# Token norms in a feature-major layer: sums and factors by transposes in place of products

## The chip, the cores and the metric

One NeuronCore of a Trainium2 chip runs the whole program. The metric is the device time of one execution in microseconds (us). Engines: TensorE (PE; its weight loads are shown apart, as PEld), VectorE (DVE), ScalarE (ACT), GpSimd (POOL) and SyncE (SP, which only issues DMAs here). Each engine works through its own queue in order and waits on semaphores for the others. The times of the kernel before are 2595.07, 2595.23 and 2595.78 us.

## What is computed

One encoder layer on 2048 prompt tokens and 64 sample tokens, in FP32, 1024 features wide. The two RMS norms at the end of the layer are what the change touches: one over the output of `w_o`, one over the residual sum.

```python
def rms_norm(x, g):
    xf = x.astype(jnp.float32)
    y = xf * lax.rsqrt(jnp.mean(xf * xf, axis=-1, keepdims=True) + EPS) * g.astype(jnp.float32)
    return y.astype(x.dtype)
...
    merged = jax.nn.sigmoid(gA) * yA + jax.nn.sigmoid(gB) * yB
    out = jnp.einsum('btd,de->bte', merged, w_o)
    x = x + rms_norm(out, g_post)
    gate = jax.nn.sigmoid(jnp.einsum('btd,de->bte', rms_norm(x, g_ple), w_ple_gate))
    x = x + jnp.einsum('btp,pd->btd', p.astype(x.dtype), w_ple_proj) * gate
```

Ahead of these stand a pre-norm with a large input projection, a gated short convolution (path A) and a chunked linear-attention scan (path B), whose outputs are gated and merged.

## The kernel before

Activations lie feature-major: 128 features on the partitions, tokens along the row. The 2112 tokens are worked in three blocks of 768, 704 and 640, each in two halves. A dense product of FP32 quality is made of three matmuls on numbers split into a high and a low part (lines 444 to 446 in the gates and in the paths, 595 to 597, 633 to 635 and 1223 to 1225 elsewhere); many of them are combined by one level of Strassen's scheme. The weights' high parts are made on ScalarE (L228, L275), their low parts on VectorE (L228) or reloaded from DRAM by SP (L276, L238).

A norm over features needs a sum over partitions. `final_norm` first adds the squares of the eight feature tiles into one tile `acc` (ScalarE squares, L732; VectorE adds, L733). `rms` is then called, once per norm, on one or two halves (`segs`):

- `col_rstd` (L711) multiplies each 128-token piece of `acc` as the stationary operand with a column of ones. The result is one column per piece in PSUM: tokens on the partitions, three columns for a half, for 384, 352 or 320 tokens alike, since pieces may overlap.
- `rstd_of` scales and adds eps on VectorE (L688), and raises to the power -1/2 on GpSimd (L691).
- `spread` (L702) multiplies each column, broadcast along the row, with the identity, so that every partition of the PSUM result holds the factor of each token.
- The result is copied out of PSUM: on ScalarE (L724) in the first two blocks, on VectorE (L722) in the last.

`final_norm` then rescales x by it (L1366), adds the residual (L1367), and after the second norm makes the split operands of the last product (L1384, L228). In the first two blocks each norm takes both halves at once, while TensorE works on the next block's gates (L444 to L446; their evictions include L458, L464, L473, L485 and L492, the sigmoids L853 and L859, and the stores L866 on GpSimd's queue). In the last block each half has its norms by itself. `spread` is also called twice at the head of the program, on row sums of x that were made without `col_rstd` (copies at L1536).

PSUM has two pools of one-bank tiles: five for the dense products (`pg`) and three for attention and small work (`pa`); the sums and the spreads take `pa` tiles. The order of the work within a queue is set by a scheduler from priorities and modelled costs; `placed()` asks that an instruction be issued behind the last matmul of a group, and `behind_all` behind given instructions. `T.transpose` is used already in the attention (L1068, L1070, L1156).

Of the kernel before, what the change touches and what calls it, by code (L numbers as in the profile page):

```python
# [10 lines left out]
F32 = mybir.dt.float32  # L11
# [3 lines left out]
ALU = mybir.AluOpType  # L15
# [3 lines left out]
P = 128  # L19
D = 1024  # L20
# [73 lines left out]
def hybrid_step(  # L94
# [17 lines left out]
    V, A, G, T, SP = nc.vector, nc.scalar, nc.gpsimd, nc.tensor, nc.sync  # L112
# [3 lines left out]
    const = ctx.enter_context(tc.tile_pool(name="const", bufs=1))  # L116
# [34 lines left out]
    def hn():  # L151
        return width[0] // 2

    def rt(n=0, dt=F32):
        t = ring.tile([P, BN + 2], dt, tag="r", name=nm("r"))
        return t if n is None else t[:, : n or width[0]]
# [4 lines left out]
    def ps_attn():  # L161
        return psa.tile([P, 512], F32, tag="pa", name=nm("pa"))
# [13 lines left out]
        T.matmul(unread[:, :P], idle, idle, start=True, stop=True)  # L176
    ident = const.tile([P, P], F32, tag="ident", name="ident")
    make_identity(nc, ident)
    ones = const.tile([P, 1], F32, tag="ones", name="ones")
    V.memset(ones, 1.0)  # L180
    mhalf = const.tile([P, 1], F32, tag="mhalf", name="mhalf")
    V.memset(mhalf, -0.5)
    vec = const.tile([P, 9, KB], F32, tag="vec", name="vec")
# [114 lines left out]
    def placed():  # L298

        return tc.issue_after(last[0]) if last[0] is not None else nullcontext()  # L300
# [35 lines left out]
    def kept_w(i1, i2, name, anew=False, spread=False):  # L336

        keys = dict(A11=(i1, 0), A12=(i1, 1), A22=(i2, 1))
        if name in keys:
            return split_w(load_raw(w_blk[keys[name]]), None if anew else keys[name], spread)  # L340
        return split_w(load_raw(sums[i1][name]), (i1, name))
# [341 lines left out]
    def tiles_of(n):  # L683

        return [(i, min(i * P, n - P)) for i in range((n + P - 1) // P)]

    def rstd_of(ms_ap, out_ap, scale, start=0):
        scaled = V.tensor_scalar(out_ap, ms_ap, scale, EPS, ALU.mult, ALU.add).ins  # L688
        means[:] = [scaled]
        shape = [out_ap.shape[0], out_ap.shape[1]]  # L690
        powers[:] = [G.tensor_tensor(out_ap, out_ap, mhalf[start : start + shape[0], :].to_broadcast(shape), ALU.pow).ins]  # L691
        return scaled

    def cols_tile(n):
        return small.tile([P, (n + P - 1) // P], F32, tag="cols", name=nm("cols"))

    def spread(cols, n):

        pb = ps_attn()
        with placed():  # L700
            for i, o in tiles_of(n):
                T.matmul(pb[:, o : o + P], cols[:, i : i + 1].to_broadcast([P, P]), ident, start=True, stop=True)  # L702
        return pb[:, :n]

    def col_rstd(acc, n):

        pc = ps_attn()
        cols = cols_tile(n)
        with placed():
            for i, o in tiles_of(n):  # L710
                T.matmul(pc[:, i : i + 1], acc[:, o : o + P], ones, start=True, stop=True)  # L711
        rstd_of(pc[:, : cols.shape[1]], cols, 1.0 / D)
        return cols

    def rms(acc, out, segs, hasten=False):


        cols = [col_rstd(acc[:, cols_of(sg)], sg["n"]) for sg in segs]
        yield
        for sg, col in zip(segs, cols):  # L720
            if hasten:
                ahead[:] = [V.tensor_copy(out[:, cols_of(sg)], spread(col, sg["n"])).ins]  # L722
            else:
                A.copy(out[:, cols_of(sg)], spread(col, sg["n"]))  # L724
        yield
# [807 lines left out]
    with behind_all(done):  # L1533
        rs = rt()
        cols = [spread(ss[:, 0, 3 * h : 3 * h + 3], hn()) for h in range(2)]
# [30 lines left out]
    for bi, bl in enumerate(blocks):  # L1566
# [10 lines left out]
        cols, a_first = [], []  # L1577
# [16 lines left out]
        mg, xo, h2, acc = [], [], [], rt()  # L1594
# [117 lines left out]
```

## Time and profile before

| | |
|---|---|
| runs | 2595.07, 2595.23, 2595.78 us, median 2595.23 |
| span of the profiled execution, first to last instruction | 2590.9 us |
| median less span: what lies around it | 4.3 us |
| granted TensorE clock | 1.000 |
| busy: ScalarE | 1530.4 us, 59% |
| busy: GpSimd | 368.3 us, 14% |
| DMA, mean of 40 slices | 286 GB/s |

The execution's own time is not listed apart from the three runs; its span stands 4.3 us below their median. In the rows that follow, a line of the timeline has the start (us from the span's start), the duration, the engine, the line of the kernel, the operation, output and input, and a count where like instructions were merged; in brackets stands how long the engine had been idle, and whom it waited for. A listing of one line gives least, median and longest duration in ns. Matmul durations overlap, so the distance from start to start is what one costs.

### The profile page before, as it was taken

What the parts mean: (1) busy time and instruction counts of PE and PEld (TensorE: products, weight loads), DVE (VectorE), ACT (ScalarE), POOL (GpSimd) and SP (SyncE); (2) the same over time, 40 slices, a digit from 0 to 9 for tenths busy, and PEclk for the clock granted to TensorE, in tenths of its full rate; (3) what the DMA queues carried; (4) which work ended last, traced back from release to release, by engine and by line L of the source; (5) the groups of instructions that cost most, each with busy time, mean ns of one, the idle gap of its engine ahead of it and who ended that gap; (6) DMA issues with size and microseconds to landing.
All of it is one profiled execution on the core that took longest, in us unless ns stands there. A gap on an engine that the chain in (4) does not pass through costs nothing.

```text
span 2590.9 us, 47524 instructions
## 1 busy us (share of the span) xinstructions
PE 2572.4 (99%) x16436; PEld 2556.1 (99%) x16436; DVE 1726.9 (67%) x3500; ACT 1530.4 (59%) x2973; POOL 368.3 (14%) x677
## 2 busy tenths in 40 slices
PE   9999999999999999999999999999999999999999
PEld 9999999999999999999999999999999999999998
DVE  7788778888777775466464556987345545336967
ACT  6766676455453764466564555566456665446675
POOL 2011111230022021111111221102100000001011
PEclk9999999999999999999999999999999999999999
DMA  8678777899897888877768998989887788999986
GB/s 325 224 262 288 263 260 273 310 360 308 262 349 238 272 311 269 281 248 233 262 227 287 342 388 313 323 291 334 295 268 251 246 273 264 299 297 323 333 270 200
DMA packets 361234, 739.87 MB, mean 286 GB/s; under 512 B 44119, under 2 KB 48785, under 8 KB 360993
## 3 DMA queue, kind: packets, MB, share of 16 engines
q1 hardware_dynamic: 321696, 582.69, 67.3%
q0 software_dynamic: 39296, 154.14, 16.3%
q8 instruction: 129, 2.11, 0.3%
q14 instruction: 113, 0.92, 0.1%
HBM read 543.44 MB, written 193.22 MB: 284 GB/s over the span
## 4 chain that ended last, share of the span: by engine, by line
PE 90%; DMA 4%; DVE 4%; issue 1%; ACT 1%; SPq 0%; POOL 0%; DVEq 0%; ACTq 0%
PE pg L444 19%; PE pg L446 19%; PE pg L445 19%; PE pg L596 5%; PE pg L595 5%; PE pg L597 5%; PE pg L635 3%; PE pg L634 3%; PE pg L633 3%; PE pa L1098 1%; PE pa L1138 1%; DMA lo<-low 1%; PE pa L1140 1%; PE pa L1084 1%; DMA low<-lo 1%
## 5 line engine op out<-in xcount | busy, mean ns | idle before, releaser
L444 PE MATMUL pg<-r,hi 128*128 128x320 f32 (+2 forms) x3304 | 1086.4, 329 | 1.4 <-DVE r L492 0.7
L445 PE MATMUL pg<-r,hi 128*128 128x320 f32 (+2 forms) x3304 | 1067.6, 323 | 0.0
L446 PE MATMUL pg<-r,lo 128*128 128x384 f32 (+2 forms) x2356 | 768.8, 326 | 5.3 <-DMA lo<-low 3.4
L275 ACT CAST hi<-raw 128x512 fp32r<-128x512 f32 x730 | 449.7, 620 | 515.5 <-PE pg L445 179.2
L444 PEld LDWEIGHTS pg<-r,hi 128*128 128x128 f32 x3304 | 621.5, 188 | 3.3 <-issue 1.0
L445 PEld LDWEIGHTS pg<-r,hi 128*128 128x128 f32 x3304 | 621.9, 188 | 0.0
L446 PEld LDWEIGHTS pg<-r,lo 128*128 128x128 f32 x2356 | 442.5, 188 | 7.9 <-DMA lo<-low 4.4
L446 PE MATMUL pg<-r,s 128*128 128x352 f32 (+1 forms) x948 | 299.4, 316 | 0.3 <-DMA s<-low 0.3
L596 PE MATMUL pg<-r,hi 128*128 128x320 f32 (+2 forms) x864 | 277.4, 322 | 0.6 <-DVE r L228 0.6
L595 PE MATMUL pg<-r,hi 128*128 128x320 f32 (+2 forms) x864 | 275.0, 322 | 0.0
L228 ACT CAST hi<-raw 128x512 fp32r<-128x512 f32 x252 | 155.6, 620 | 155.5 <-PE pg L445 44.0
L228 DVE TENSOR_TENSOR r<-r,r 128x320 fp32r<-128x320 f32 (+7 forms) x354 | 208.7, 608 | 52.9 <-ACT r L228 51.3
L228 ACT CAST r<-r 128x320 fp32r<-128x320 f32 (+7 forms) x354 | 185.9, 557 | 57.0 <-DMA r<-w_blk 13.0
L228 DVE TENSOR_TENSOR lo<-raw,hi 128x512 fp32r<-128x512 f32 x231 | 157.9, 685 | 88.0 <-ACT hi L228 84.2
L597 PE MATMUL pg<-r,lo 128*128 128x352 f32 (+2 forms) x564 | 180.9, 321 | 0.7 <-DMA lo<-low 0.7
L446 PEld LDWEIGHTS pg<-r,s 128*128 128x128 f32 x948 | 177.9, 188 | 0.7 <-DMA s<-low 0.6
L228 ACT CAST hi<-s 128x512 fp32r<-128x512 f32 x156 | 96.2, 618 | 120.1 <-PE pg L445 102.0
L634 PE MATMUL pg<-r,hi 128*128 128x384 f32 (+2 forms) x512 | 166.8, 326 | 0.2 <-DVE r L228 0.2
L633 PE MATMUL pg<-r,hi 128*128 128x384 f32 (+2 forms) x512 | 166.3, 328 | 0.2 <-ACT hi L275 0.2
L596 PEld LDWEIGHTS pg<-r,hi 128*128 128x128 f32 x864 | 162.2, 188 | 2.4 <-DVE r L228 1.7
L595 PEld LDWEIGHTS pg<-r,hi 128*128 128x128 f32 x864 | 161.3, 188 | 1.3 <-ACT r L228 0.6
L458 ACT COPY hf<-pg 128x352 f32<-128x352 f32 (+2 forms) x354 | 157.1, 446 | 1.7 <-PE pg L446 1.3
(403 smaller groups left out, 4114.3 us busy)
## 6 DMA issues: line engine op xcount, KB each, us to landing
raw<-w_blk SPq DMA_DIRECT2D x577, 256.0 KB, 4.1
raw<-S SPq DMA_DIRECT2D x444, 256.0 KB, 4.2
lo<-low SPq DMA_DIRECT2D x422, 256.0 KB, 4.1
s<-low SPq DMA_DIRECT2D x308, 256.0 KB, 4.0
low<-lo SPq DMA_DIRECT2D x271, 256.0 KB, 3.8
S<-s SPq DMA_DIRECT2D x152, 256.0 KB, 3.6
low<-r POOLq DMA_DIRECT2D x54, 256.0 KB, 5.1
r<-w_blk POOLq DMA_DIRECT2D x52, 256.0 KB, 6.9
```

The lines of the kernel that those rows point to most:

```text
L228: return A.copy(hi, src).ins, V.tensor_tensor(lo, src, hi.bitcast(F32), ALU.subtract).ins
L275: A.copy(hi, raw)
L444: add(hi[:, k, :], xhi, start=start and k == 0, stop=False)
L445: add(hi[:, k, :], xlo, start=False, stop=False)
L446: last[0] = add(lo[:, k, :], xhi, start=False, stop=k == KH - 1).ins
L458: copied = A.copy(got[n], ps[bank])
L595: add(hi[:, k, :], xhi, start=start and k == 0, stop=False)
L596: add(hi[:, k, :], xlo, start=False, stop=False)
L597: last[0] = add(lo[:, k, :], xhi, start=False, stop=k == KH - 1).ins
L633: T.matmul(ps, hi[:, k % 4, :], xhi[:, c], start=k == ks[0], stop=False)
L634: T.matmul(ps, hi[:, k % 4, :], xlo[:, c], start=False, stop=False)
L635: last[0] = T.matmul(ps, lo[:, k % 4, :], xhi[:, c], start=False, stop=k == ks[-1]).ins
```

## The change

The sums over features no longer come from a product with ones. Each 128x128 piece of `acc` is transposed by TensorE into PSUM, so that tokens lie on the partitions and the partial sums of 128 features along the row, and VectorE adds along the row, three pieces in one instruction. `rstd_of` then reads and writes the small tile in SBUF in place of PSUM. The spread's product of a broadcast column with the identity becomes a transpose of the broadcast column. The tile of ones goes.

```diff
-    ones = const.tile([P, 1], F32, tag="ones", name="ones")
-    V.memset(ones, 1.0)
...
             for i, o in tiles_of(n):
-                T.matmul(pb[:, o : o + P], cols[:, i : i + 1].to_broadcast([P, P]), ident, start=True, stop=True)
+                T.transpose(pb[:, o : o + P], cols[:, i : i + 1].to_broadcast([P, P]), ident)
...
             for i, o in tiles_of(n):
-                T.matmul(pc[:, i : i + 1], acc[:, o : o + P], ones, start=True, stop=True)
-        rstd_of(pc[:, : cols.shape[1]], cols, 1.0 / D)
+                T.transpose(pc[:, i * P : i * P + P], acc[:, o : o + P], ident)
+        count = cols.shape[1]
+        V.tensor_reduce(cols, pc[:, : count * P].rearrange("p (i c) -> p i c", c=P), axis=mybir.AxisListType.X, op=ALU.add)
+        rstd_of(cols, cols, 1.0 / D)
         return cols
```

## The prediction

> **What bounds the kernel now.** I read the page first: busy shares by engine, then the chain that ended last.
>
> ```profile
> PE 2572.4 (99%) x16436; PEld 2556.1 (99%) x16436; DVE 1726.9 (67%) x3500; ACT 1530.4 (59%) x2973; POOL 368.3 (14%) x677
> PE 90%; DMA 4%; DVE 4%; issue 1%; ACT 1%; SPq 0%; POOL 0%; DVEq 0%; ACTq 0%
> ```
>
> TensorE is busy 99% of the span and 90% of the chain; VectorE has a third of its time free. So time taken off TensorE's queue shortens the run, and time put on VectorE costs only where TensorE comes to wait for it. Matmul durations overlap, so I price TensorE by the distance between starts, on the row of weight loads, and look at each place where a norm is made. There are seven stretches: H, the head (two spreads of the already finished row sums); A1 and A2, the two norms of the first block (each two sums, then two spreads); B1 and B2 of the second block; and in the third block four single norms C1 to C4 in order of time, each of one half of the tokens.
>
> ```profile
> L711 PE MATMUL pa<-ones,r x72: 164/250/271, 911.9 to 2545.6; 128*128 128x1 f32 x72
> L702 PE MATMUL pa<-ident,cols x72: 270/275/376, 915.1 to 2549.6; 128*128 128x128 f32 x72
> ```
>
> The listing of one line shows 72 records for L711; the code issues 36 products there, so an FP32 product is two records. L702 has 36 too, and 6 more in the head. 78 products become transposes.
>
> **Removed: the price of a product against a transpose.** Weight loads in A2 (start, duration, line):
>
> ```profile
> 958.03 1.47 PEld L711 LDWEIGHTS pa<-ones,r 128*128 128x128 f32 x12
> 959.41 0.19 PEld L444 LDWEIGHTS pg<-r,hi 128*128 128x128 f32 x1
> 959.52 0.19 PEld L445 LDWEIGHTS pg<-r,hi 128*128 128x128 f32 x1
> 959.69 0.19 PEld L446 LDWEIGHTS pg<-r,s 128*128 128x128 f32 x1
> ```
>
> From 958.03 to 959.52 lie six products and one ordinary matmul (0.16 to 0.17): 1.49 - 0.16 = 1.33 us, 0.222 each. The trace of before holds transposes of the same size in the attention (L1156, one record each):
>
> ```profile
> 123.79 0.53 PEld L1156 LDWEIGHTS pa<-ident,r 128*128 128x128 f32 x4
> 124.29 0.19 PEld L444 LDWEIGHTS pg<-r,hi 128*128 128x128 f32 x1
> 124.40 0.19 PEld L445 LDWEIGHTS pg<-r,hi 128*128 128x128 f32 x1
> 124.57 0.19 PEld L446 LDWEIGHTS pg<-r,lo 128*128 128x128 f32 x1
> ```
>
> Four transposes and one matmul (0.17) in 0.61: 0.44, or 0.11 each. Each edit saves 0.112 us, six save 0.67, three 0.34, and all 78 save 8.7. That is the most that TensorE can gain.
>
> A rule speaks against this: the Trainium skill, "TensorE: Matmul & The Clock Gate", Part 4: PE-mode transpose, gives about 275 ns for a 128x128 transpose inside a kernel, and says that transposes don't count as activity for the clock gate. If that were their spacing, the change would cost 78 x (0.275 - 0.222) = 4.1 us, an estimate from that page; the trace has starts 0.11 us apart, so by the row the rule's figure is a latency. No run here shows what a long row of transposes does to the clock; these come in threes and sixes among matmuls.
>
> **Added: a reduction on VectorE.** Twelve sums over three rows of 128, read from PSUM. The two nearest reductions, from SBUF:
>
> ```profile
> L1149 DVE TENSOR_REDUCE ms<-r 128x4 f32<-128x512 f32 x16 | 11.0, 687 | 27.9 <-ACT r L1148 27.9
> L1149 DVE TENSOR_REDUCE ms<-one 128x1 f32<-128x128 f32 x16 | 4.5, 279 | 0.0
> ```
>
> The second number behind the bar is the mean in ns. It is 408 ns for 384 more elements, so 384 take 279 + 272 = 551 ns. Bounds 0.28 and 0.69; I take 0.55. Twelve of them are 6.6 us of VectorE, nothing beside its 860 free, but each lies between the sums and the factors. `rstd_of` (scale on VectorE, power on GpSimd) stays, and so does the copy out of PSUM. The ones tile and its memset go, worth nothing: VectorE sets up while TensorE does its idle products.
>
> **Where the reduction meets TensorE.** In the changed program's order the queues are alike but for the places below. VectorE does reduce, reduce, scale, L473, scale, and at A1 and B1 GpSimd now issues one L866 store between its two powers. The second scale waits behind L473, which waits for a ScalarE copy (bound: nothing to 0.4). In SP's order five loads move by one to three places; I count that as nothing, covered by the weights already loaded for the matmuls ahead of them, and one stall of 2.9 (rival 2) is the price if that cover is gone. The spread waits for the power; behind it on TensorE stand the dense matmuls of the next gates, and for those the evictions on ScalarE and VectorE. A1:
>
> ```profile
> 911.86 1.42 PEld L711 LDWEIGHTS pa<-ones,r 128*128 128x128 f32 x12 [0.40 <-DVE r L733]
> 912.75 0.52 DVE L492 TENSOR_TENSOR r<-hf,hf 128x352 f32<-128x352 f32 x1
> 913.19 0.37 DVE L688 TENSOR_SCALAR cols<-pa 128x3 f32<-128x3 f32 x2
> 913.43 1.72 POOL L691 TENSOR_TENSOR cols<-cols,mhalf 128x3 f32<-128x3 f32 x2 [28.33 <-DVE cols L688]
> 915.11 0.61 POOL L866 DMA_DIRECT2D g__2774_11267<-r  x1
> ```
>
> Six transposes from 911.86 end at 912.52. VectorE is free at 913.19; two reductions end at 914.29; the power starts 0.24 behind the scale (913.43 - 913.19), lasts 0.86, and ends at 915.39; TensorE starts 0.05 later (as in C2 below, 2521.54 to 2521.59), 915.44. The new order has 13 matmuls before the first spread (11 before), at 0.161 each (A2: 963.24 - 958.03 less 1.33, over 24): 912.52 + 2.10 = 914.62, a wait of 0.82. Then the spread, 0.33, and five matmuls, 0.81: 916.58. The second power starts behind the store, 916.00, and is there at 916.91: 0.33 more. Of 1.34 saved, 1.15 is given back: -0.2.
>
> B1, with matmuls of 0.147 (C3: 2525.55 - 2523.11 less 0.67, over 12):
>
> ```profile
> 1758.78 1.41 PEld L711 LDWEIGHTS pa<-ones,r 128*128 128x128 f32 x12 [0.35 <-DVE r L733]
> 1759.04 0.48 DVE L492 TENSOR_TENSOR r<-hf,hf 128x320 f32<-128x320 f32 x1
> 1762.43 0.60 POOL L866 DMA_DIRECT2D g__5173_21796<-r  x1 [0.82 <-ACT r L859]
> ```
>
> VectorE is free at 1759.48 (0.44 behind that L492, as in A1), reductions go to 1760.58, power to 1761.69. The slot, ten matmuls behind the transposes, is 1758.78 + 0.66 + 1.47 = 1760.91: wait 0.82. The second power stands behind a store that waits for a ScalarE row. If that row comes 0.65 earlier with TensorE, the wait is 0.5; if not, 1.15. I take the first: net 0.0 (bound +0.6).
>
> B2, and the spread of A2:
>
> ```profile
> 1798.61 1.45 PEld L711 LDWEIGHTS pa<-ones,r 128*128 128x128 f32 x12
> 1800.88 0.22 DVE L688 TENSOR_SCALAR cols<-pa 128x3 f32<-128x3 f32 x2
> 963.24 1.46 PEld L702 LDWEIGHTS pa<-ident,cols 128*128 128x128 f32 x12
> 1803.47 1.45 PEld L702 LDWEIGHTS pa<-ident,cols 128*128 128x128 f32 x12
> ```
>
> In B2 VectorE comes to the sums only at 1800.88; reductions to 1801.98, first power to 1803.09. The slot moves up to 1802.80: wait 0.34, then 0.54 for the second power. Net -0.5. A2 has 5.2 us from 958.03 to 963.24, 4.5 after the change; sums 0.66, hand-over 0.22, reductions 1.1, 0.24, two powers 1.72: 4.0. No wait, -1.34.
>
> C2 and C3, by short windows of each engine:
>
> ```profile
> 2519.55 0.74 PEld L711 LDWEIGHTS pa<-ones,r 128*128 128x128 f32 x6 [0.31 <-DVE r L733]
> 2521.59 0.74 PEld L702 LDWEIGHTS pa<-ident,cols 128*128 128x128 f32 x6 [0.50 <-POOL cols L691]
> 2523.11 0.78 PEld L711 LDWEIGHTS pa<-ones,r 128*128 128x128 f32 x6
> 2525.55 0.78 PEld L702 LDWEIGHTS pa<-ident,cols 128*128 128x128 f32 x6
> 2520.42 0.16 DVE L688 TENSOR_SCALAR cols<-pa 128x3 f32<-128x3 f32 x1 [0.92 <-PE pa L711]
> 2520.66 0.88 POOL L691 TENSOR_TENSOR cols<-cols,mhalf 128x3 f32<-128x3 f32 x1 [18.89 <-DVE cols L688]
> 2524.09 1.00 DVE L1384 SCALAR_TENSOR_TENSOR r<-r,vec,r 128x320 f32<-128x320 f32 x2
> 2524.26 1.09 POOL L691 TENSOR_TENSOR cols<-cols,mhalf 128x3 f32<-128x3 f32 x1 [2.72 <-DVE cols L688]
> ```
>
> TensorE waits 0.50 here already. C2: the scale comes 0.33 sooner for the transposes and 0.55 later for the reduction, 2520.64; spread at 2521.81 instead of 2521.59, done at 2522.14 instead of 2522.26 with seven matmuls before it, not six. C3: six matmuls later transposes end at 2523.35, the reduction at 2524.12 (0.22 of hand-over, as 2520.42 stands behind the end of the sums at 2520.21). The new order then puts both L1384 (1.00) ahead of the scale: 2525.12, power 2525.36 to 2526.43, spread done at 2526.81 instead of 2526.22. The slot was 2523.35 + 13 x 0.147 = 2525.26, so TensorE waits 1.1. Less the two matmuls now done earlier (0.29), C2 and C3 lose 0.3 where they would have saved 1.34.
>
> C1 and C4 have slack:
>
> ```profile
> 2495.76 0.78 PEld L711 LDWEIGHTS pa<-ones,r 128*128 128x128 f32 x6
> 2499.07 0.78 PEld L702 LDWEIGHTS pa<-ident,cols 128*128 128x128 f32 x6
> 2545.05 0.74 PEld L711 LDWEIGHTS pa<-ones,r 128*128 128x128 f32 x6 [0.39 <-DVE r L733]
> 2548.91 0.78 PEld L702 LDWEIGHTS pa<-ident,cols 128*128 128x128 f32 x6
> ```
>
> After the change 3.0 and 3.5 us lie from sums to spread. C1 needs 0.33 + 0.22 + 0.55 + 0.24 + 0.88, and 0.5 for the L620 that the new order puts between reduction and scale (priced like one L1384): 2.7. C4 needs 2.4 with the power of 1.09. No wait, -0.67 each. The head has only spreads, no new chain: -0.67.
>
> **The sum:** H -0.67, A1 -0.19, A2 -1.34, B1 0.0, B2 -0.46, C1 -0.67, C2 with C3 +0.30, C4 -0.67: -3.7 us. The profiled span is 2590.9, the median of the runs 2595.2; the 4.3 around the span are not touched. So span 2587.2, time 2591.5.
>
> **The rivals.**
> (1) *Everything is kept.* The waits above rest on VectorE reaching the sums when it did before; where it is sooner, or the waits use up later ones, the whole 8.7 stays: 2586.5. For it: few TensorE waits for VectorE in the whole trace. Against: the 0.50 wait at 2521.59.
> (2) *Slower: the late factors block VectorE's queue.* The rescaling of x (L1366) waits for the spread, and evictions that free TensorE's PSUM banks stand behind it. It decides where lateness exceeds the bank slack. Price: the 1.2 us of A1 once more at A1, B1, B2 and C3, plus one more stall of weights like the longest of this group:
>
> ```profile
> PEld pg L446 <- DMA lo<-low: 4.4, 4, 2.9
> ```
>
> -3.7 + 4.8 + 2.9 = +4.0, 2599.2; with another such stall 2602. Against: the pool has five banks, and at A1 the new order puts the eviction L464 ahead of the first L1366, and L485 behind two of them instead of three.
> (3) *Transposes cost their duration.*
>
> ```profile
> L1156 PE MATMUL pa<-ident,r x112: 270/272/302, 124.0 to 2178.2; 128*128 128x128 f32 x112
> ```
>
> 0.272 is 0.05 more than a product: 78 x 0.05 = +3.9, 2599.1; the waits would be no longer than above, since TensorE comes to them later. It is the mechanism of the rule named above. The spacing of 0.11 speaks against it.
> (4) *It doesn't do what it says*: the compiled transposes of a broadcast column are two records as before. Then 42 spreads save nothing (4.7 us less): +1.0, 2596.2.
>
> **How the numbers follow.** Forecast 0.48, (1) 0.36, (2) 0.11, (3) 0.02, (4) 0.03. The likeliest is 2591.5. Its own unknowns: B1 +0.6, the reduction at 0.69 instead of 0.55 some +1.0 in five waits, at 0.28 some -2; one longer or vanished DMA stall 2.9: 2587 to 2596. Together with (1) the range is 2585.0 to 2598.0. The mark of 0.2% (what a measurement can tell from no change) is 5.2 us: faster means below 2590.0. (1) and the low edge of the forecast make 0.40; slower is (2) where the second stall of weights comes in, and what no case names, 0.10; 0.50 is left.
>
> **What would show it.** L711's successor and L702 with half as many records, starts 0.11 us apart. Twelve reductions near 0.55 us. TensorE waits for GpSimd of 0.8 and 0.3 at A1, the like at B1, 0.9 in C2, 1.1 in C3, none in A2. Wrong would be: reductions over 0.7 us, no such waits (then rival 1), or new waits of TensorE for evictions within 15 us behind A1 and B1 (rival 2).

## The result, and the profile after

| | before | after |
|---|---|---|
| runs of this comparison, median | 2595.23 us (2594.28 to 2596.14, 5 runs) | 2584.25 us (2581.3 to 2587.84, 5 runs) |
| ratio after to before | | 0.9968, 95% interval 0.9956 to 0.998 |
| span of the profiled execution | 2590.9 us | 2579.6 us (its time: 2581.3, the fastest of the five) |

The change makes the kernel faster, by 11.0 us between the medians. The forecast was 3.7 us, and the median lies 0.75 us below the low edge of the range. The recorded ratio, 0.9968, is not the quotient of these two medians, which is 0.9958: by the ratio the change is worth 8.3 us and the time is 2586.9, inside the range. The record does not say how the ratio was formed. Either way the kernel gained more than was forecast, so the question for the experiments is where the other 5 to 7 us come from.

The page of after, top lines and the chain that ended last:

```profile
span 2579.6 us, 47382 instructions
PE 2562.4 (99%) x16358; PEld 2546.4 (99%) x16358; DVE 1733.2 (67%) x3511; ACT 1529.9 (59%) x2973; POOL 369.5 (14%) x677
PE 86%; issue 5%; DVE 4%; DMA 3%; ACT 1%; POOL 1%; SPq 0%; DVEq 0%; POOLq 0%; ACTq 0%
```

TensorE has 78 records fewer (16436 less 16358): each of the 78 edits dropped one. VectorE has 6.3 us more, and 11 instructions more: twelve reductions less the memset of the ones. "issue" rose from 1% to 5% of the chain, which looks like lost time and isn't. The chain of after around A1 (start, duration, piece):

```profile
880.02 0.54 POOL r L1348
880.56 30.02 issue
910.58 0.02 POOLq L866
...
910.62 0.64 POOL cols L689
...
913.24 0.54 PE pa L700 x3
```

Going back from the spread (L700), the chain steps over to GpSimd, since TensorE waited for its power (L689), and then follows GpSimd's own queue back through 30 us in which GpSimd had nothing to do. TensorE worked through those 30 us. A like piece of 26.0 us stands ahead of B1; the two are some two thirds of the rise. What is new is that the chain steps over to GpSimd at A1, B1, B2, C2 and C3, where in before it did so at C2 alone.

The listings of the new lines in after (least, median, longest in ns):

```profile
L711 DVE TENSOR_REDUCE cols<-pa x12: 548/554/558, 909.4 to 2535.0; 128x3 f32<-128x384 f32 x12
L700 PE MATMUL pa<-ident,cols x36: 270/273/323, 911.8 to 2538.2; 128*128 128x128 f32 x36
L689 POOL TENSOR_TENSOR cols<-cols,mhalf x12: 845/1050/1107, 910.6 to 2535.8; 128x3 f32<-128x3 f32 x12
```

A reduction takes 0.55 us, and the spreads of the norms are 36 records where they were 72. What TensorE waits for, summed over the whole program, first in before and then in after (us in total, times, longest):

```profile
PEld pa L702 <- POOL cols L691: 0.5, 1, 0.5
```

```profile
PEld pa L700 <- POOL cols L689: 5.8, 8, 1.1
```

This is the price of the reductions: 5.3 us more of waiting for the factors. 78 edits at 0.112 are 8.7 us, less 5.3 is 3.4. The places, by weight loads of after at A1, B1, B2 and then C2 and C3:

```profile
908.11 0.64 PEld L709 LDWEIGHTS pa<-ident,r 128*128 128x128 f32 x6 [1.01 <-DVE r L733]
...
911.76 0.30 PEld L700 LDWEIGHTS pa<-ident,cols 128*128 128x128 f32 x3 [0.87 <-POOL cols L689]
...
913.24 0.30 PEld L700 LDWEIGHTS pa<-ident,cols 128*128 128x128 f32 x3 [0.42 <-POOL cols L689]
...
1753.21 0.30 PEld L700 LDWEIGHTS pa<-ident,cols 128*128 128x128 f32 x3 [0.90 <-POOL cols L689]
...
1754.70 0.30 PEld L700 LDWEIGHTS pa<-ident,cols 128*128 128x128 f32 x3 [0.48 <-POOL cols L689]
...
1793.55 0.30 PEld L700 LDWEIGHTS pa<-ident,cols 128*128 128x128 f32 x3 [0.38 <-POOL cols L689]
1794.59 0.30 PEld L700 LDWEIGHTS pa<-ident,cols 128*128 128x128 f32 x3 [0.74 <-POOL cols L689]
...
2511.01 0.30 PEld L700 LDWEIGHTS pa<-ident,cols 128*128 128x128 f32 x3 [1.06 <-POOL cols L689]
...
2515.59 0.30 PEld L700 LDWEIGHTS pa<-ident,cols 128*128 128x128 f32 x3 [0.94 <-POOL cols L689]
```

And A2, where nothing waits:

```profile
952.40 0.74 PEld L709 LDWEIGHTS pa<-ident,r 128*128 128x128 f32 x6
...
956.93 0.73 PEld L700 LDWEIGHTS pa<-ident,cols 128*128 128x128 f32 x6
```

To see what each stretch is worth, I compared the distance between the same two dense weight loads in both kernels. All kernels of this study have 16280 weight loads outside the sums and the spreads. They come in the same order, but for at most 30 that change places inside A1, B1 and C2 with C3, so at the bounds of every stretch the n-th load is the same piece of work. Differences to the profile of before shown above, in us, by the prediction's names. It counts seven stretches, but names nine places, and as C2 and C3 share one row here there are eight; they are called the norm stretches below, and the seven stretches in the expectations:

| stretch (time in before) | forecast | after | after, 2nd profile | after, 3rd profile |
|---|---|---|---|---|
| H (20 to 30) | -0.67 | -0.43 | -0.43 | -0.49 |
| A1 (908 to 925) | -0.19 | +0.42 | -0.22 | -0.21 |
| A2 (955 to 975) | -1.34 | -1.37 | -1.37 | -1.37 |
| B1 (1757 to 1772) | 0.0 | -0.15 | -0.09 | -0.17 |
| B2 (1797 to 1815) | -0.46 | -0.31 | -0.64 | -0.29 |
| C1 (2490 to 2503) | -0.67 | -0.65 | -0.67 | -0.67 |
| C2 and C3 (2517 to 2530) | +0.30 | +0.08 | +0.07 | +0.08 |
| C4 (2543 to 2553) | -0.67 | -0.64 | -0.62 | -0.62 |
| together | -3.7 | -3.0 | -4.0 | -3.7 |
| 545 to 582, no norm in it | 0 | -3.4 | -2.8 | -3.8 |
| all the rest, no norm in it | 0 | -4.9 | -0.8 | -2.5 |

The norms gave about what was forecast. The remainder of the first profile's 11 us lies where the two kernels do the same work in the same order on TensorE, and the largest piece of it is at 545 to 582. TensorE's waits there, of before and then of after:

```profile
PEld pg L446 <- DVE lo L228: 3.3, 5, 1.4
PEld pg L444 <- issue: 1.0, 1, 1.0
```

```profile
PEld pg L442 <- issue: 0.7, 1, 0.7
PEld pg L444 <- DVE lo L226: 0.2, 1, 0.2
```

In before TensorE waits five times for low parts of weights (L228, the same line as L226 in after); in after once.

### The profile page after: what moved, and what is told of

It reads as the page before. It is cut to its first block, busy times and chain, and to the rows that moved or that the text cites. A ratio compares the mean times of both kernels' runs of the same rounds, so it can differ in the third digit from the quotient of the medians.

```text
span 2579.6 us, 47382 instructions
## 1 busy us (share of the span) xinstructions
PE 2562.4 (99%) x16358; PEld 2546.4 (99%) x16358; DVE 1733.2 (67%) x3511; ACT 1529.9 (59%) x2973; POOL 369.5 (14%) x677
## 4 chain that ended last, share of the span: by engine, by line
PE 86%; issue 5%; DVE 4%; DMA 3%; ACT 1%; POOL 1%; SPq 0%; DVEq 0%; POOLq 0%; ACTq 0%
PE pg L442 18%; PE pg L443 18%; PE pg L444 18%; PE pg L594 4%; PE pg L593 4%; PE pg L595 4%; PE pg L633 3%; PE pg L632 3%; PE pg L631 3%; PE pa L1098 1%; PE pa L1138 1%; PE pa L1140 1%; PE pa L1084 1%; DMA lo<-low 1%; DVE lo L226 1%
## 5 line engine op out<-in xcount | busy, mean ns | idle before, releaser
L226 ACT CAST hi<-raw 128x512 fp32r<-128x512 f32 x252 | 155.5, 620 | 155.8 <-PE pg L443 40.0
L226 DVE TENSOR_TENSOR r<-r,r 128x320 fp32r<-128x320 f32 (+7 forms) x354 | 209.5, 611 | 51.9 <-ACT r L226 50.4
L226 ACT CAST r<-r 128x320 fp32r<-128x320 f32 (+7 forms) x354 | 185.8, 557 | 54.4 <-DMA r<-w_blk 10.9
L226 DVE TENSOR_TENSOR lo<-raw,hi 128x512 fp32r<-128x512 f32 x231 | 158.7, 689 | 86.8 <-ACT hi L226 81.5
L226 ACT CAST hi<-s 128x512 fp32r<-128x512 f32 x156 | 96.3, 618 | 123.9 <-PE pg L443 107.4
```

What stands on the lines that cost most here:

```text
L226: return A.copy(hi, src).ins, V.tensor_tensor(lo, src, hi.bitcast(F32), ALU.subtract).ins
```

## The experiments

Three groups of kernels ran, each with its own runs of before beside it; the median of before was 2591.2, 2589.3 and 2590.2 us, its single runs from 2584.8 to 2600.6. Every kernel has 12 timed runs and one profile. "Norms" is the sum over the eight norm stretches, "545" the stretch from 545 to 582, "rest" what is left of the difference at the last weight load; all three are us against the first profile of before. The expectations were written down with absolute times counted from the first comparison; since before is 4 to 6 us lower in these groups, only their differences can be held against the results.

| kernel | median (range), us | ratio to before, 95% interval | norms | 545 | rest |
|---|---|---|---|---|---|
| spreads alone | 2586.12 (2582.93 to 2589.83) | 0.998, 0.997 to 0.999 | -3.9 | -1.7 | -1.9 |
| sums alone | 2591.14 (2586.78 to 2595.91) | 0.9997, 0.9987 to 1.0006 | +1.5 | +0.5 | -1.2 |
| head kept as products | 2586.36 (2583.84 to 2591.65) | 0.9984, 0.9975 to 0.9993 | -3.3 | -3.6 | +0.8 |
| head alone | 2588.68 (2587.03 to 2595.88) | 0.9996, 0.9987 to 1.0005 | -0.6 | -0.9 | -3.1 |
| after again | 2586.27 (2581.05 to 2587.67) | 0.9983, 0.9973 to 0.9993 | -4.0 | -2.8 | -0.8 |
| before again | 2590.34 (2583.47 to 2594.44) | 1.000, 0.9987 to 1.0012 | +0.1 | -0.3 | -6.3 |
| mixed | 2583.17 (2579.56 to 2586.29) | 0.9976, 0.9966 to 0.9986 | -5.4 | -2.2 | -0.5 |
| each reduction twice | 2588.92 (2585.01 to 2592.52) | 0.9994, 0.9984 to 1.0004 | -3.2 | -0.8 | +1.3 |
| after, third | 2585.52 (2581.69 to 2590.11) | 0.9979, 0.9968 to 0.9991 | -3.7 | -3.8 | -2.5 |
| mixed again | 2583.77 (2580.28 to 2588.17) | 0.9975, 0.9965 to 0.9985 | -5.6 | -4.0 | -2.8 |
| before, third | 2592.42 (2587.97 to 2598.23) | 1.0006, 0.9996 to 1.0016 | +0.6 | -3.1 | +4.8 |

### Spreads alone

The factors by transposes, the sums by products with ones as in before.

```diff
-                T.transpose(pc[:, i * P : i * P + P], acc[:, o : o + P], ident)
-        count = cols.shape[1]
-        V.tensor_reduce(cols, pc[:, : count * P].rearrange("p (i c) -> p i c", c=P), axis=mybir.AxisListType.X, op=ALU.add)
-        rstd_of(cols, cols, 1.0 / D)
+                T.matmul(pc[:, i : i + 1], acc[:, o : o + P], ones, start=True, stop=True)
+        rstd_of(pc[:, : cols.shape[1]], cols, 1.0 / D)
```

> Only the spreads are transposes (42 of them); the sums stay products with ones, no reduction. By the prices of the prediction: 42 x 0.112 = -4.7 us at the norms, with no new wait of TensorE for GpSimd except a longer one in C2 (0.5 before). Theory S (the head, 0.7 us shorter, shifts all that follows, and the waits of TensorE between 545 and 580 us go with the shift): a further -3.4 us there, 2587 in all. Theory R (those waits come and go from run to run): at the head -0.7, between 545 and 580 nothing that holds in all runs, 2590.

TensorE's waits for the factors in this kernel:

```profile
PEld pa L702 <- POOL cols L691: 0.7, 2, 0.5
```

0.2 us more than in before, for 42 edits: 4.7 saved, less 0.2 of waits, less 0.2 at the head (below) is 4.3, and the norm stretches show 3.9. Half of the change already gives all that the whole change gives at the norms. The stretch from 545 to 582 came out at -1.7, between theory S (-3.4) and theory R, and does not decide between them.

### Sums alone

The reverse: sums by transposes and a reduction, spreads by products.

```diff
-                T.transpose(pb[:, o : o + P], cols[:, i : i + 1].to_broadcast([P, P]), ident)
+                T.matmul(pb[:, o : o + P], cols[:, i : i + 1].to_broadcast([P, P]), ident, start=True, stop=True)
```

> Only the sums are transposes with a reduction; the spreads and the head stay products. At the norms -4.0 by the transposes and about 3 given back in waits for GpSimd at A1, B1, B2, C2 and C3: -1. Theory S: no shift before A1, so the waits between 545 and 580 stay (4 us of them), 2594. Theory R: they may be gone in the profiled run though nothing ahead of them has changed.

```profile
PEld pa L700 <- POOL cols L689: 5.7, 8, 1.0
```

36 edits save 4.0 us, and 5.2 us of new waits are put in: +1.2, and the norm stretches show +1.5 (A1 +0.92, B1 +0.68, B2 +0.30, C2 and C3 +0.85, against A2 -0.69, C1 -0.33, C4 -0.29). The waits of the changed kernel belong to this half of the change. Its time is the same as before within its interval.

### The head: kept as products, and alone

The first kernel is after with the two spreads of the head as products; the second is before with those two as transposes.

```diff
-    def spread(cols, n):
+    def spread(cols, n, head=False):
...
+                if head:
+                    T.matmul(pb[:, o : o + P], cols[:, i : i + 1].to_broadcast([P, P]), ident, start=True, stop=True)
+                else:
...
-        cols = [spread(ss[:, 0, 3 * h : 3 * h + 3], hn()) for h in range(2)]
+        cols = [spread(ss[:, 0, 3 * h : 3 * h + 3], hn(), True) for h in range(2)]
```

> The changed kernel with its two spreads at the head made by products again; the six matmuls are all that differs. Theory S: the waits between 545 and 580 are back, 0.7 + 3.4 slower than the changed kernel in the profile, about 2588 to 2589 in the median. Theory R: 0.7 slower only, about 2585.

> The kernel before with only the two spreads at the head as transposes. Theory S: -0.7 at the head and -3.4 between 545 and 580, 2591. Theory R: -0.7, 2594.5.

Apart from the memset of the ones, the head's edit is the only part of the change ahead of 545 us, so if the change itself removed the waits at 545 to 582, this would have to be its cause. It isn't: without it that stretch is 3.6 us shorter, with it alone 0.9. Of the six spreads' 0.67 us at the head 0.43 arrive. The weight loads of after show why:

```profile
23.78 0.74 PEld L700 LDWEIGHTS pa<-ident,rows 128*128 128x128 f32 x6
24.67 0.19 PEld L1223 LDWEIGHTS pa<-r,r 128*128 128x128 f32 x1 [0.15 <-ACT r L1230]
```

The load behind the spreads now waits 0.15 us for a ScalarE row, for which no wait shows in before; that is most of the 0.24 that are missing.

### After again, before again

Both kernels unaltered, in one group.

> The changed kernel once more, unaltered. Theory P (the change is worth what it does at the norms; the first profile gained the rest in waits on DMAs that differ from run to run): about -3 at the norms in the trace again, a median some 3 to 5 us under the kernel before, and another sum in the stretches 545 to 582, 935 to 950, 1500 to 1535 and 1776 to 1790. Theory Q (the change itself removes those waits): 10 to 11 us under the kernel before, with the same four stretches as short as in the first profile.

> The kernel before once more, unaltered. Theory P: the four stretches differ from the first profile of it by some us in all, the norms by less than 0.1 us each; ratio 1.000. Theory Q: the four stretches are as in its first profile.

The norm stretches of after come out as in its first profile, but for A1 (+0.42 there, -0.22 here) and B2. But the same program of before, run again, ended 6.4 us sooner than in its first profile (span 2584.5 against 2590.9), with nothing changed at the norms (+0.1). So stretches outside the norms move by nearly as much as the whole surplus of the first comparison. One stretch shows it in both directions: 935 to 950 is 1.7 us shorter than in the first profile of before in after, 1.8 us longer in after again, and 1.9 us shorter in before again. TensorE's waits there are on transfers, in the first profile of before and in after again:

```profile
PEld pg L446 <- DMA lo<-low: 2.9, 1, 2.9
```

```profile
PEld pg L444 <- DMA lo<-low: 2.7, 1, 2.7
PEld pg L444 <- DMA s<-low: 0.5, 1, 0.5
```

The waits alone don't explain it: they are 2.9 us in the one and 3.2 in the other, and the stretch is 1.8 us longer. The rest goes with the granted clock of TensorE. 935 to 950 in each of the same two profiles' own time (window, length, busy time of each engine, then granted clock, DMA share and GB/s):

```profile
935.00:950.00 15.00, 12.40 (x77) 12.10 (x77) 11.46 (x16) 8.57 (x16) 2.69 (x5) 1.00 1.01 371
```

```profile
935.00:950.00 15.00, 12.40 (x66) 11.85 (x65) 9.93 (x15) 7.65 (x15) 2.16 (x4) 0.89 0.99 366
```

In after again the clock was halved for some 3.4 us, and matmuls there start 0.29 us apart, not 0.16:

```profile
941.31 0.49 PE L442 MATMUL pg<-r,hi 128*128 128x352 f32 x1
941.60 0.50 PE L443 MATMUL pg<-r,hi 128*128 128x352 f32 x1
```

That is about 1.5 us lost, an estimate from these two distances; with the 0.3 us more of waits it makes up the 1.8. Five of the thirteen profiles have such a dip in this stretch (after again, the third of before, sums alone, head kept as products, each reduction twice). In them the stretch is 1.0 to 2.1 us longer than in the first profile of before; in the other seven, at 1.00, it is 0.2 to 1.9 shorter. Two more dips stand elsewhere, at 576 in sums alone and at 1784 in each reduction twice. All seven begin within 1.4 us behind the end of a TensorE wait of 2.0 to 2.9 us. But five waits of 2.2 to 2.9 us have no dip behind them, that of the first profile of before among them, and what decides is not shown.

### Before and after for a third time

In two profiles of after the stretch from 545 to 582 had been short, and in two of before long. That left it open whether the change shortens it by a way that I had not seen.

> The changed kernel once more, unaltered, for a third profile. In two profiles of it the stretch from 545 to 582 us is 3.4 and 2.8 us shorter than in the first profile of before, in one further profile of before 0.3 us shorter. Theory P (what the change is worth is its seven stretches, 3 to 4 us; the rest is waits on transfers that differ from run to run): 3 to 4 us below the before of this call, the seven stretches again -3 to -4 together, 545 to 582 anywhere between 0 and -3.5. Theory Q (the change itself also removes the waits at 545 to 582): that stretch again 2.8 to 3.4 shorter, and 6 to 7 us below before.

> The kernel before once more, unaltered, for a third profile. Theory P: its stretch from 545 to 582 us falls anywhere between 0 and -3.5 against its first profile, and its span lies between 2584 and 2591. Theory Q: the stretch is long, within 0.5 us of the first profile, as in both profiles of before so far.

TensorE's waits at 545 to 582 in the third profile of before:

```profile
PEld pg L446 <- DVE lo L228: 1.0, 2, 0.5
PEld pg L444 <- issue: 0.7, 1, 0.7
```

The unaltered kernel before has the short stretch too: -3.1 us, with 1.0 us of waits for the low parts in place of 3.3. The change is not needed for it, and theory Q falls. Theory P did not come out whole either: the stretch of after, -3.8, lies just beyond its bound. In this profile of before C2 with C3 is 0.45 us longer, where TensorE waits 0.8 us for the last addition of squares (L733; 0.3 in the first profile), so sums over the norm stretches can differ by 0.6 with no edit at all. Elsewhere TensorE lost time to transfers, the clock dipped at 943, and the span was 2593.2, the longest of all and above the 2591 that theory P allowed:

```profile
PEld pg L446 <- DMA lo<-low: 4.6, 4, 2.9
PEld pg L597 <- DMA lo<-low: 3.7, 2, 2.2
PEld pg L446 <- DMA s<-low: 2.8, 5, 0.8
```

The span of before is 2590.9, 2584.5 and 2593.2 in three profiles, that of after 2579.6, 2583.4 and 2580.9.

### Each reduction twice

After with every reduction issued twice, which doubles its 0.55 us. The result is the same; the time is that of 24 reductions.

```diff
-        V.tensor_reduce(cols, pc[:, : count * P].rearrange("p (i c) -> p i c", c=P), axis=mybir.AxisListType.X, op=ALU.add)
+        for _ in range(2):
+            V.tensor_reduce(cols, pc[:, : count * P].rearrange("p (i c) -> p i c", c=P), axis=mybir.AxisListType.X, op=ALU.add)
```

> The changed kernel with every reduction done twice, into the same columns: 0.55 to 0.6 us more on VectorE between each sum and its factor, 1.2 where a norm has two. If the reduction sits on TensorE's path at A1, B1, B2, C2 and C3 and in slack at A2, C1 and C4: +1.2 at A1, +1.2 at B1, +1.2 at B2, +0.55 at C2 and at C3 each, 0 at C4, 0.3 to 0.6 at A2 and at C1, whose slack is about used up: some +5 in all. If VectorE's part is hidden everywhere: no site moves.

If the wait at a norm were the reduction's length alone, A1 and B1 would have grown, by 1.1 us each. They shrank: A1 is 0.60 us shorter than in before (0.2 in the second and third profiles of after), B1 0.86 (0.1 to 0.2). Weight loads of this kernel at A1, B1 and C1:

```profile
909.34 0.64 PEld L709 LDWEIGHTS pa<-ident,r 128*128 128x128 f32 x6 [0.37 <-DVE r L734]
...
913.72 0.30 PEld L700 LDWEIGHTS pa<-ident,cols 128*128 128x128 f32 x3 [0.49 <-POOL cols L689]
...
1759.38 0.30 PEld L700 LDWEIGHTS pa<-ident,cols 128*128 128x128 f32 x3 [0.60 <-POOL cols L689]
...
1761.41 0.36 PEld L700 LDWEIGHTS pa<-ident,cols 128*128 128x128 f32 x3
...
2496.15 0.30 PEld L700 LDWEIGHTS pa<-ident,cols 128*128 128x128 f32 x3 [0.82 <-POOL cols L689]
```

At A1 the factors come 4.4 us behind the sums (909.34 to 913.72) where they came 3.65 us behind them in after (908.11 to 911.76), yet TensorE waits less. The scheduler knew of the longer chain and placed the first spread 20 dense matmuls behind the sums, not 13; at B1 17, not 10. So the wait at A1 and B1 is the distance between the slot, the place that the order gives to the spread, and the factor, and in after the slot is too early. Where the slot did not move, the longer chain is paid: at C1, with 18 matmuls in both kernels, 0.82 us of wait where there was none. C2 and C3 lose 1.2 us more than in after, most of it in another wait, of a weight load for a ScalarE split (L226) whose input VectorE makes (0.3 us in after):

```profile
2522.85 0.30 PEld L631 LDWEIGHTS pg<-r,hi 128*128 128x128 f32 x2 [1.23 <-ACT r L226]
```

So the simple expectation, more reduction, more wait at every short norm, was wrong for A1, B1 and B2 and right for C1 and for C2 with C3. In all the norm stretches give -3.2, 0.8 us less than after in the same group, where 5 were expected.

### Mixed: a version that takes only what pays

Factors by transposes everywhere. Sums by transposes where the norm has slack (A2, C1, C4), by products with ones where TensorE would wait (A1, B1, B2, C2, C3).

```diff
+                if slack:
+                    T.transpose(pc[:, i * P : i * P + P], acc[:, o : o + P], ident)
+                else:
+                    T.matmul(pc[:, i : i + 1], acc[:, o : o + P], ones, start=True, stop=True)
...
-        yield from rms(acc, rs, segs, bl["last"])
+        yield from rms(acc, rs, segs, bl["last"], bl["last"] and not ask_ahead)
...
-        yield from rms(acc2, rs2, segs, bl["last"])
+        yield from rms(acc2, rs2, segs, bl["last"], segs[0] is bl["segs"][0] and bl["t0"] == 0 or ask_ahead)
```

> Spreads by transposes everywhere; sums by transposes and a reduction only where the trace has slack for it (A2, C1, C4), by products with ones in A1, B1, B2, C2 and C3. By the sites measured so far: head -0.4, A1 -0.45, A2 -1.4, B1 -0.55, B2 -0.65, C1 -0.65, C2 and C3 -0.45, C4 -0.65: -5.2 at the norms against -3.1 of the changed kernel, so 2 us faster than it, if the waits elsewhere are alike. If sums by transposes had lost nothing at A1, B1, B2, C2 and C3, it would be 2.7 slower than the changed kernel.

> Factors by transposes everywhere, sums by transposes only at A2, C1 and C4, the rest of the sums by products with ones, once more. Theory P: the seven stretches sum to -5 to -5.5 as in its first profile, so 1 to 2.5 us below the changed kernel of this call, with the waits of TensorE for GpSimd absent at A1, B1, B2 and C3 and 0.5 at C2. Rival (its lead of 3 us in the first call was chance): the same time as the changed kernel within 1 us, though the stretches are shorter.

TensorE's waits for the factors, over the whole program, and the spread of A1 in the first profile of it:

```profile
PEld pa L702 <- POOL cols L691: 0.6, 2, 0.5
```

```profile
910.04 1.41 PEld L714 LDWEIGHTS pa<-ones,r 128*128 128x128 f32 x12 [0.37 <-DVE r L739]
...
913.11 0.73 PEld L702 LDWEIGHTS pa<-ident,cols 128*128 128x128 f32 x6
```

54 edits at 0.112 are 6.0 us, less 0.1 of waits for factors, less 0.2 at the head: 5.7, and the norm stretches show 5.4 and 5.6. Its median is 3.1 and 1.8 us below that of after in the same group. The intervals of the two ratios overlap, so the times alone don't separate them; the norm stretches do, in both profiles. By them it is the best version of this study. Part of the lead in time may be the clock's: every run's granted clock is on record, and 19 of this kernel's 24 runs had 1.000, but 9 of the 24 of after. Among these the means are 2583.0 and 2583.4 against 2583.1 and 2583.9, which shows no lead, though so few runs can't exclude one of 2 us. Whether the kernel itself brings fewer dips was not tested.

## Why the prediction was right or wrong

**The price of an edit** held. Transposes start 0.11 us apart in the new code (six in 0.61 at A1, from 908.11 to the next load at 908.72), products 0.22. The sums of saved records and new waits agree with the stretches within half a microsecond in spreads alone, sums alone and mixed. By the rule of the Trainium skill that the prediction set beside this ("TensorE: Matmul & The Clock Gate", Part 4: PE-mode transpose, about 275 ns each), the spreads alone would have been slower, by 42 times 0.053 (0.275 less 0.222), 2.2 us, an estimate from that page; that kernel is faster (0.997 to 0.999). The page's figure, measured there in bf16, agrees with the duration of an FP32 record here, 0.273 us, not with the spacing. Rival 3 falls with it, and rival 4 by the 36 records where there were 72.

**The reduction** was estimated at 0.55 us from two reductions out of SBUF; out of PSUM it measured 0.554.

**The waits** came where they were named. A1: 0.87 and 0.42 against 0.8 and 0.3; B1: 0.90 and 0.48 against 0.82 and 0.5; B2: 0.38 and 0.74 against 0.34 and 0.54; C2 and C3: 1.06 and 0.94 against 0.9 and 1.1 (C3 is 1.2 by the prediction's own rows: 2526.43 and 0.05, less 2525.26); none at A2, C1 and C4. In the second profile of after B2's first wait is gone, which is its -0.64. The first profile's A1 is 0.6 us worse than the others because its sums came late: TensorE waited 1.01 us there for the last addition (L733), 0.40 in before. The second profile has 0.37 at that place.

**The head** gave 0.2 us less than forecast, for the wait on ScalarE that the prediction left out; C2 with C3 came out 0.2 better, B1 0.1.

**Rival 1**, everything is kept, gave 2586.5 and is nearest to the measured time, but not by its mechanism: it needs the waits for the factors to be absent, and they are there, 5.3 us of them. A time that fits a rival doesn't confirm it.

**Rival 2**, late factors that block evictions, did not happen: in after TensorE waits for nothing over the 15 us behind A1's last spread, nor behind B1's.

**The weakest step** is the width given to all that lies outside the norms: "one longer or vanished DMA stall 2.9". I took that size from the longest stall of one profile, and the three runs at hand agreed within 0.7 us, so I held the rest of the kernel for fixed. It isn't: two profiles of the unaltered kernel before differ by 8.7 us in span, and its 35 runs in the second group by 12.6 us. Several stalls move at once, and a stall can bring a clock dip, which costs some 1.5 us more.

**The base** was not safe either. The prediction took the 4.3 us between span and median for time that lies around the span. In every later run time less span is 1.6 to 1.8 us, so the profiled execution of before took about 2592.6, less than all five runs of the first comparison. And these five, with a median of 2595.23, lie 4 to 6 us above the medians of the same kernel in the three groups, while the first 2584.25 of after lies only 1.3 and 2.0 below its later medians. Of the 99 runs of before in the groups 14 are as long as the shortest of those five. So most of what the first comparison shows beyond the forecast lies in its runs of before; why they were longer the record does not show. In the two groups that ran after again its median is 3.1 and 4.6 us below that of before, near the forecast.

**What stays open.** Runs with the same granted clock can be compared: at 1.000 after is 4.8 us below before in both of these groups (means of 4 and 18 runs, of 5 and 11), at 0.999 5.0 and 4.6 (7 and 14, 7 and 15). The 95% interval of each reaches 1.9 to 2.5 us to either side. This is a check and not an experiment, since stalls bring the dips. The norm stretches show 3.0 to 4.0, so about 1 us is left, which is within that uncertainty and within the 0.6 us by which the unaltered kernel's norm stretches moved. Two stretches without a norm differ alike in all three profiles of after, 975 to 1450 by -0.25 and 1815 to 2360 by +0.35; they cancel. Whether stalls or dips are fewer with the change, three profiles of each kernel, each several microseconds apart, can't tell.

## What to carry to other kernels

Price a small TensorE operation by the distance between starts, and price its replacement by the chain that it makes longer: here an edit that was pure gain (the spreads) was bound up with one that was a loss at five of eight places (the sums), and only running them apart, or reading each place's slack, shows it. Take the longer form where there is slack and the shorter chain where the next engine is waiting. Before reading a difference of a few microseconds as the change's, profile the unaltered kernel twice: stretches that move between two profiles of one program belong to nobody's edit. Look at the granted clock of each such stretch too: 0.999 over the whole span can be 3.4 us at half clock in one place.

## What had not been expected of the hardware

One program's span differs by 8.7 us between profiles (2584.5 to 2593.2) with much of the difference in waits on transfers and on what they feed: 545 to 582 moved by 3 us, 935 to 950 by 4. The granted clock, 1.000 and 0.999, looks alike and is not: the 0.999 hides 3.4 us at half clock behind a stall of 2.9 us. Over the 123 runs of before in the three groups the mean is 2588.7 us at 1.000, 2592.1 at 0.999 and 2595.2 at 0.998. And making the reduction twice as long shortened two of the norms, since the order is planned ahead: the engine's wait depends on where the plan put the next instruction as much as on how long the work takes.
